# Output projection, norm and first feed-forward products of a two-layer backbone, by halves of the tokens

## The chip, the cores and the metric

The kernel runs on one core of a Trainium2 chip. The metric is the time of one execution on the device in microseconds (us); before the change it is 2305.74 us (median of three runs, 2302.88 to 2308.2).

## What is computed

Two layers over 512 latent tokens and 256 context tokens of width D = 1024, in float32. Layer 0 mixes tokens by attention, layer 1 by a bidirectional RWKV-7 scan; layer 1 updates the latents alone. Each mixer ends in an output projection `wo`, whose result is added by a gate; then comes a modulated RMS norm and a SwiGLU network (DFF = 2816), added by a gate too. Cut to what matters here:

```python
y, yc = mixer(h, hc, ...)                     # ends in o @ wo, o (tokens, 1024), wo (1024, 1024)
x = x + m[:, 2] * y
h2 = rmsnorm(x, norm2_g[i]) * (1.0 + m[:, 4]) + m[:, 3]
x = x + m[:, 5] * ((silu(h2 @ wg) * (h2 @ wu)) @ wd)
# layer 0: the same for the context tokens, with their own modulation
```

## The kernel before

Features lie on the 128 partitions, tokens along a row: `xT` is [128, 8 feature tiles k, tokens], and a copy of it is kept in DRAM (`xd`). Every product is made of three float32r passes, of high and low parts (xh wh, xl wh, xh wl), so a weight block [128, 4, 128] becomes a "unit": a raw tile `wr` (0.5 MB loads of line 249 on SyncE's queue, SP, four buffers), a CAST to the high part on ScalarE (ACT, line 239) and a difference for the low part (line 241), which goes to VectorE (DVE), for every third unit to GpSimd (POOL). Seven units can be held.

The part that is changed runs once per layer. It starts when the mixer's output stands in SBUF as `oTh`, `oTl` (line 726 is attention's last cast):

- `out_project` (from line 264) forms wo^T o in eight feature tiles, all tokens of a tile before the next one (the two streams of 512 and 256 tokens apart; the last two tiles by halves of the tokens). Line 228 is the matmul, 258 adds by the gate on DVE, 277 writes to `xd`.
- `squares` (lines 176, 178) sums x * x over the feature tiles, for either half of the tokens; line 186 sums over partitions by matmul, 158 to 165 form the inverse root, 194 and 197 spread it over the partitions (`rbp`).
- `norm_blocks` (from line 300) multiplies by the inverse norm (314, DVE), modulates (322 on ACT for the first half of the tokens, 320 on POOL for the second), and forms the seven token blocks of a Strassen-Winograd product: B11 and B21 of the first half (x1, x2), B22 and T1 to T4, which need both halves (x3 to x7). Their sums are 336, 339, 341 and 344, each over four feature tiles, on POOL; 329 and 330 split each block into high (ACT) and low (DVE) parts.
- `ffn` (from line 349) takes pairs of feature tiles b = 0 to 10: `gate_up(b)` makes the seven products of gate and up weights (line 395, in the order 1, 2, 5, 6, 7, 3, 4, in PSUM tiles A, B, C); sums of weight blocks are line 360 on POOL; 383 to 404 combine products on DVE and ACT, with Silu at 404. `down` (429) follows one pair behind.

Half n2 is 384 tokens in layer 0 and 256 in layer 1. A list scheduler puts the instructions of each engine in their order when the kernel is built; each engine then runs its own list in order, as SP does with its loads. The output projection is called at line 744 (layer 0, after the load of `xT` at 736) and 1408 (layer 1); `mods`, a pool of two 1 MB tiles `mw`, holds the modulation weights that are loaded during attention (line 123).

## Time and profile before

| | |
|---|---|
| median of three runs | 2305.74 us (2302.88 to 2308.2) |
| span of the profiled execution | 2302.6 us; its time outside the span isn't recorded, and the span is 3.1 us below the median |
| busy share PE, DVE, ACT, POOL | 88%, 73%, 48%, 34% |
| chain that ended last: PE, DVE | 63%, 20% |
| layer 0, end of attention to the second pair's products | 429.5 to 600.1 us |
| layer 1, end of the readout to the second pair's products | 1863.3 to 2004.8 us |

PE is TensorE's matmuls. The chain is the row of pieces that ended last, followed back from the last instruction; a window gives each engine's busy time in one stretch, with the granted clock of TensorE as a share of its full 2.4 GHz. In a timeline, what stands in brackets is the idle time of the engine before the instruction and what ended it. One execution is profiled, so durations come from that one.

### The profile page before, as it was taken

The page shows a single profiled execution, that of the slowest core. Times are in us where ns is not written, and L with a number is a line of the kernel's source. Part 1 is how long each engine was busy: PE and PEld are TensorE (multiplying, and loading weights), DVE is VectorE, ACT ScalarE, POOL GpSimd, SP SyncE. Part 2 cuts the span into 40 slices and gives each one's busy share as a digit, 9 for nine tenths or more (in the row PEclk, how much of TensorE's full clock was granted, in tenths as well). Part 3 has the DMA queues.
Part 4 walks back from the last instruction along what each step waited for, and adds up shares of the span by engine and source line. Part 5 has one row for each costly group of instructions (what it writes and reads, how often), then busy time and mean ns, then how long its engine had stood idle before and what let it go on. Part 6 is the DMA issues. An engine that isn't in the chain of part 4 may idle for free.

```text
span 2302.6 us, 42745 instructions
## 1 busy us (share of the span) xinstructions
PE 2034.6 (88%) x16422; PEld 1779.6 (77%) x16422; DVE 1669.9 (73%) x3382; ACT 1094.9 (48%) x2276; POOL 790.8 (34%) x663
## 2 busy tenths in 40 slices
PE   6999999797999999995988978767888777899998
PEld 4995555586999999994767956656777666899998
DVE  4565556449877777768465597798888758988896
ACT  5446656434333333335343764765664534444443
POOL 1110000027434443423142531552430325666661
PEclk7999999998999999997988979778889987999999
DMA  8206660421321222111326543432321631433332
GB/s 298 67 25 222 237 237 21 148 91 48 109 74 63 74 68 74 62 55 64 100 88 211 148 121 120 121 107 64 110 62 54 189 121 47 138 97 97 105 97 74
DMA packets 178714, 247.94 MB, mean 108 GB/s; under 512 B 16808, under 2 KB 109968, under 8 KB 178128
## 3 DMA queue, kind: packets, MB, share of 16 engines
q1 hardware_dynamic: 177792, 244.37, 33.0%
q8 instruction: 130, 2.13, 0.4%
q10 hardware_dynamic: 352, 0.60, 0.1%
q0 software_dynamic: 368, 0.26, 0.1%
q14 instruction: 72, 0.59, 0.1%
HBM read 199.04 MB, written 33.55 MB: 101 GB/s over the span
## 4 chain that ended last, share of the span: by engine, by line
PE 63%; DVE 20%; ACT 5%; issue 5%; DMA 4%; POOL 2%; SPq 1%; DVEq 0%; ACTq 0%; POOLq 0%
PE yps L429 13%; PE A L395 8%; PE C L395 5%; PE B L395 5%; PE yps L228 5%; PE po L724 3%; DVE O L1144 3%; PE pj L228 3%; PE S L705 2%; DVE E L1147 2%; PE PTp L719 2%; PE mps L126 2%; DVE wu L241 2%; PE qps L578 2%; PE qps L580 2%
## 5 line engine op out<-in xcount | busy, mean ns | idle before, releaser
L429 PE MATMUL yps<-gh,wu 128*128 128x384 f32 (+2 forms) x1120 | 323.4, 345 | 3.7 <-DVE xT L258 3.6
L258 DVE SCALAR_TENSOR_TENSOR xT<-yps,modT,xT 128x384 f32<-128x384 f32 (+2 forms) x348 | 183.9, 548 | 134.1 <-PE yps L429 95.0
L241 POOL TENSOR_TENSOR wu<-wr,wu 128x512 fp32r<-128x512 f32 x77 | 107.1, 1392 | 472.6 <-ACT wu L239 456.9
L239 ACT CAST wu<-wr 128x512 fp32r<-128x512 f32 x252 | 154.6, 620 | 222.2 <-PE A L395 66.4
L429 PEld LDWEIGHTS yps<-gh,wu 128*128 128x128 f32 x1120 | 201.6, 188 | 16.5 <-DVE xT L258 4.7
L239 ACT CAST wu<-ws 128x512 fp32r<-128x512 f32 x176 | 108.0, 620 | 200.2 <-PE yps L429 86.5
L241 DVE TENSOR_TENSOR wu<-wr,wu 128x512 fp32r<-128x512 f32 x175 | 157.7, 903 | 50.8 <-ACT wu L239 47.8
L429 PE MATMUL yps<-gl,wu 128*128 128x384 f32 (+2 forms) x560 | 192.1, 344 | 0.0
L360 POOL TENSOR_TENSOR ws<-wr 128x512 f32<-128x512 f32 x88 | 130.1, 1482 | 165.8 <-DMA wr<-in_ffn_wg_dram 71.5
L241 DVE TENSOR_TENSOR wu<-ws,wu 128x512 fp32r<-128x512 f32 x111 | 125.8, 1139 | 9.8 <-ACT wu L239 9.8
L241 POOL TENSOR_TENSOR wu<-ws,wu 128x512 fp32r<-128x512 f32 x65 | 88.1, 1356 | 90.3 <-ACT wu L239 87.6
L429 PEld LDWEIGHTS yps<-gl,wu 128*128 128x128 f32 x560 | 105.4, 188 | 4.5
L228 PE MATMUL yps<-oTh,wu 128*128 128x512 f32 (+2 forms) x416 | 101.6, 347 | 8.2 <-ACT wu L239 8.2
L708 DVE TENSOR_REDUCE mx<-S 128x1 f32<-128x768 f32 (+1 forms) x96 | 74.7, 778 | 44.4 <-PE S L705 43.7
L720 ACT COPY PT<-PTp 128x384 f32<-128x384 f32 (+1 forms) x160 | 69.3, 465 | 54.0 <-PE PTp L719 53.8
L395 PE MATMUL C<-x5h,wu 128*128 128x384 f32 (+1 forms) x352 | 85.6, 318 | 6.0 <-ACT x5h L329 5.2
L719 PEld LDWEIGHTS PTp<-ident,pr 128*128 128x128 f32 x448 | 50.2, 144 | 50.5 <-issue 23.6
L395 PE MATMUL A<-x1h,wu 128*128 128x384 f32 (+1 forms) x352 | 88.0, 315 | 1.1 <-ACT x1h L329 1.1
L395 PE MATMUL B<-x2h,wu 128*128 128x384 f32 (+1 forms) x352 | 83.8, 310 | 4.7 <-ACT x2h L329 4.6
L1147 DVE TENSOR_TENSOR E<-E,O 128x110 f32<-128x110 f32 (+22 forms) x288 | 84.2, 325 | 0.3
L395 PE MATMUL A<-x6h,wu 128*128 128x384 f32 (+1 forms) x352 | 83.1, 314 | 1.0 <-DVE wu L241 1.0
L1144 DVE TENSOR_TENSOR O<-E 128x110 f32<-128x110 f32 (+22 forms) x288 | 82.4, 322 | 1.9
(408 smaller groups left out, 6365.4 us busy)
## 6 DMA issues: line engine op xcount, KB each, us to landing
mw<-in_mod_w_dram SPq DMA_DIRECT2D x48, 1024.0 KB, 5.3
wr<-in_ffn_wg_dram SPq DMA_DIRECT2D x44, 512.0 KB, 3.8
wr<-in_ffn_wu_dram SPq DMA_DIRECT2D x44, 512.0 KB, 3.6
wr<-in_ffn_wd_dram SPq DMA_DIRECT2D x44, 512.0 KB, 3.9
wraw<-in_rwkv_wrkv_dram SPq DMA_DIRECT2D x32, 256.0 KB, 3.1
wraw<-in_attn_wqkv_dram SPq DMA_DIRECT2D x12, 512.0 KB, 4.5
xT<-xd SPq DMA_DIRECT2D x2, 3072.0 KB, 9.8
AR<-lw SPq DMA_DIRECT2D x48, 128.0 KB, 2.3
```

The lines of the kernel that those rows point to most:

```text
L228: nc.tensor.matmul(ps, w(k), x(k, sl), start=(k == 0 and i == 0), stop=(k == nk - 1 and i == 2))
L239: nc.scalar.copy(hi, raw)
L241: (nc.gpsimd if lane["n"] % 3 == 0 else nc.vector).tensor_tensor(out=lo, in0=raw, in1=hi, op=ALU.subtract)
L258: nc.vector.scalar_tensor_tensor(out=xT[:, f, t0:t1], in0=ps[:, t0 - sl.start:t1 - sl.start], scalar=modT[:, l, 8 * m + f, s:s + 1], in1=x ...
L360: nc.gpsimd.tensor_tensor(out=t, in0=x, in1=y, op=op)
L395: nc.tensor.matmul(ps, w[:, k], x[:, k], start=(k + j == 0), stop=(k == 3 and j == 2))
L429: nc.tensor.matmul(ps, u[k // 2][w][:, k % 2, fs], gs[k // 2][x][:, k % 2, sl], start=(k + j == 0), stop=(k == nk - 1 and j == 2))
L708: nc.vector.tensor_reduce(out=mx, in_=S[:, :nk * P], axis=AX.X, op=ALU.max)
L719: nc.tensor.transpose(ps[:, t - t0, :], pr_[:, P * t:P * t + P], ident)
L720: nc.scalar.copy(PT[h][:, t0:t1, P * qt:P * qt + P], ps[:, :t1 - t0, :])
L1144: nc.vector.tensor_tensor(out=tv, in0=E[:, a_:b, s:s + 1].to_broadcast([P, b - a_, m]), in1=E[:, s:s + 1, :s].to_broadcast([P, b - a_, m]) ...
L1147: nc.vector.tensor_tensor(out=E[:, a_:b, :s], in0=E[:, a_:b, :s], in1=tv, op=ALU.add)
```

## The change

- The projection runs by halves of the tokens: eight feature tiles of the first half, then eight of the second (`out_half`). Weights are loaded and cast again for the second half.
- In layer 0 the weights of the first two blocks (2 x 1 MB) are loaded through the modulation weights' buffers, on SP ahead of the load of `xT`.
- `norm_half` norms the first half of the tokens and splits x1 and x2 beside the second half's projection. For the second half, modulation is on ACT (it was on POOL), and the token sums are on DVE, in pieces of one (line 323) or two feature tiles (333).
- `gate_first` runs products 1 and 2 of the pairs b = 0 and 1 (8 x 12 = 96 matmuls), which need the first half alone, behind the projection; their weights come in 256 KB loads. `gate_up` makes the other five products. All PSUM tiles are in one pool.

```diff
-    def out_project(wp, pl, xT, src, xh, xl, l, m, n):
...
+    def out_half(wp, pf, xT, src, xh, xl, l, m, sl, ready=None):
+        tags = [f"{z}{y}" for z in "ABC" for y in range(2)]
+        w = sl.stop - sl.start
         for b in range(4):
...
+            rw_ = (ready or {}).get(b) or raws(wp, src, 256 * b, 256)
+            for q in range(2):
                 f = 2 * b + q
...
+                us = [unit(wp, r[:, :, P * q:P * q + P], (4, P)) for r in rw_]
+                ps = pf.tile([P, 512], F32, name="yps", tag=tags[f % 6])[:, :w]
+                product([(ps, sl)], lambda k: us[k // 4][0][:, k % 4], lambda k: us[k // 4][1][:, k % 4], xh, xl, KT)
+                add_gated(xT, ps, l, m, f, sl)
+                nc.sync.dma_start(out=xd[:, f, sl], in_=xT[:, f, sl])
...
-    def norm_blocks(pool, pf, xT, sums, l, w, xv, n):
...
+    def norm_half(pool, pf, xT, th, l, w, xv, n):
...
+        sl = slice(n2 * th, n2 * th + n2)
+        acc = squares(pool, xT, sl, abufs=2, bufs=2)
+        ps = pf.tile([P, 512], F32, name="rbp", tag=f"D{th}")
+        r = rms_cols(pool, ps[:, 508:512], [acc], nt)
...
+        rb = ps[:, :n2]
+        if th:
+            preload(AF.Silu, r[:, 0:1])
...
-                        if th:
-                            nc.gpsimd.tensor_scalar(out=h[:, k, t0:t1], in0=h[:, k, t0:t1], scalar1=a_, scalar2=b_, op0=ALU.mult, op1=ALU.add)
-                        else:
-                            nc.scalar.activation(h[:, k, t0:t1], h[:, k, t0:t1], AF.Identity, bias=b_, scale=a_)
...
-        nc.gpsimd.tensor_tensor(out=B11, in0=B12, in1=B11, op=ALU.subtract)
-        parts(5, B11, 2)
...
+        def normed(k):
+            nc.vector.tensor_tensor(out=xT[:, k, sl], in0=xT[:, k, sl], in1=rb, op=ALU.mult)
+            for s, off, wd in STREAMS:
+                t0, t1 = max(off, sl.start), min(off + wd, sl.stop)
+                if t0 < t1:
+                    nc.scalar.activation(xT[:, k, t0:t1], xT[:, k, t0:t1], AF.Identity, bias=modT[:, l, 8 * m + k, s:s + 1],
+                                         scale=aT[:, 2 * l + w, k, s:s + 1])
...
+        if th == 0:
+            for k in range(KT):
+                normed(k)
+                parts(1 + k // 4, (B11, B21)[k // 4], k % 4, k % 4 + 1)
+            return
+        for k in range(4):
+            normed(k)
+            nc.vector.tensor_tensor(out=B11[:, k], in0=B12[:, k], in1=B11[:, k], op=ALU.subtract)
+            parts(5, B11, k, k + 1)
+        for k in range(4):
+            normed(4 + k)
+        two = [slice(0, 2), slice(2, 4)]
+        for i, o, x, y in ((6, B11, B22, B11), (7, B12, B22, B12), (4, B21, B21, B11)):
...
+            for z in two:
+                nc.vector.tensor_tensor(out=o[:, z], in0=x[:, z], in1=y[:, z], op=ALU.subtract)
+                parts(i, o, z.start, z.stop)
...
+        def gate_first(b):
+            st = half_tiles(b, b % 2)
+            st["get"] = [first_blocks(z, b) for z in (wg, wu)]
+            gate_steps(st, ORDER[:2])
+            return st
...
+        ahead = [gate_first(b) for b in range(2)]
         for b in range(nb):
-            gs.append(gate_up(b))
+            gs.append(gate_up(b, ahead[b] if b < 2 else None))
...
+            ready = {}
+            for b in range(2):
+                raw = md.tile([P, KT, 256], F32, name="mw", tag="mw", bufs=2)
+                nc.sync.dma_start(out=raw, in_=a["attn_wo"][0].rearrange("(k p) f -> p k f", p=P)[:, :, 256 * b:256 * b + 256])
+                ready[b] = [raw[:, 0:4], raw[:, 4:8]]
...
+            for th in range(2):
+                out_half(wp, pf, xT, a["attn_wo"][0], lambda k, sl: oTh[:, k, sl], lambda k, sl: oTl[:, k, sl], 0, 2,
+                         slice(n2 * th, n2 * th + n2), None if th else ready)
...
+                norm_half(tp, pf, xT, th, 0, 1, xv, T)
```

TensorE, layer 0, behind the projection (`yps`); `acc` and `sq` are the sums of squares of half 1, `x1h` to `x2l` parts of half 0:

```order
L228 MATMUL yps<-oTh,wu 128x384
L186 MATMUL rbp<-ones,acc 128x1
L186 MATMUL rbp<-ones,sq 128x1
...
L197 MATMUL rbp<-dg,ones 128x128 x6
L395 MATMUL A_5360<-x1h,wu 128x384
L395 MATMUL A_5377<-x1h,wu 128x384
```

```order
L395 MATMUL A_5446<-x1h,wu 128x384 x2
L186 MATMUL rbp<-ones,sq 128x1
...
L395 MATMUL A_5446<-x1l,wu 128x384
...
L395 MATMUL A_5513<-x1h,wu 128x384 x2
L197 MATMUL rbp<-dg,ones 128x128 x3
L395 MATMUL A_5513<-x1l,wu 128x384
```

Before (first piece) both halves' sums and spreads stood ahead of all products; now (second piece) the sums and the spread of half 1 stand inside the first products.

SP's queue, layer 0, at the load of the projection's weights, before and then after:

```order
L123 DMA mw<-in_mod_w_dram 128x4x512 x40
L736 DMA xT<-xd 128x6144
L249 DMA wr<-in_attn_wo_dram 128x4x256 x8
L277 DMA xd<-xT 128x512
L277 DMA xd<-xT 128x256
```

```order
L707 DMA mw<-in_attn_wo_dram 128x8x256 x2
L759 DMA xT<-xd 128x6144
L249 DMA wr<-in_attn_wo_dram 128x4x256 x4
L275 DMA xd<-xT 128x384 x2
L249 DMA wr<-in_attn_wo_dram 128x4x256
L275 DMA xd<-xT 128x384
```

Two loads of the projection's weights moved ahead of the load of `xT`; the others now stand between the writes of `xd`.

ACT, layer 1, at the inverse norm (`rs_y` is the square root), before and then after:

```order
L176 ACTIVATE sq<-xT 128x256 x3
L158 ACTIVATE rs_y<-rbp,epst 128x2 x2
L153 ACT_TABLE_LOAD
L153 ACTIVATE idle<-rr,epst 128x1
L322 ACTIVATE xT<-xT,modT,aT 128x256 x2
```

```order
L239 CAST wu<-wr 128x512
L404 ACT_TABLE_LOAD
L404 ACTIVATE gt<-gt 128x256
L158 ACT_TABLE_LOAD
L158 ACTIVATE rs_y<-rbp,epst 128x2
L239 CAST wu<-ws 128x512
L398 COPY gt<-A_20170 128x256
L153 ACT_TABLE_LOAD
```

The first Silu of the feed-forward network moved ahead of half 1's square root, with a table load on either side.

## Rows read from the trace of the kernel before

**Rows 1.** The page: busy time, share of the span and instructions of each engine, and the chain that ended last, by engine.

```profile
PE 2034.6 (88%) x16422; PEld 1779.6 (77%) x16422; DVE 1669.9 (73%) x3382; ACT 1094.9 (48%) x2276; POOL 790.8 (34%) x663
...
PE 63%; DVE 20%; ACT 5%; issue 5%; DMA 4%; POOL 2%; SPq 1%; DVEq 0%; ACTq 0%; POOLq 0%
```

**Rows 2.** Windows of layer 0, from the start of the projection on: start:end, its us, then busy us and count of PE, of PE's weight loads, DVE, ACT and POOL, the granted clock as a share, the busy share of the DMA engines and GB/s.

```profile
437.65:506.80 69.15, 69.14 (x387) 62.39 (x387) 29.06 (x41) 19.57 (x35) 16.95 (x12) 0.98 0.36 119
506.80:531.20 24.40, 16.78 (x79) 15.85 (x80) 18.26 (x44) 14.94 (x27) 13.87 (x18) 0.72 0.17 52
531.20:560.10 28.90, 15.88 (x74) 14.28 (x73) 28.32 (x16) 10.54 (x18) 22.96 (x10) 0.82 0.00 1
```

**Rows 3.** The chain of work that ended last, in order of time, 420 to 605 us: start, duration, what.

```profile
425.98 10.98 DMA wr<-in_attn_wo_dram
...
524.90 3.08 POOL xT L320 x5
...
548.83 3.56 DVE x7l L330 x2
552.67 6.19 DVE x6l L330 x2
...
583.48 4.16 PE A L395 x24
```

**Rows 4.** The products of line 395 alone, from the end of attention to the second pair's products in layer 0: the window, its us, PE busy and count, then weight loads, clock, DMA.

```profile
429.50:600.12 170.62, 64.63 (x336) 61.59 (x336) 0.91 0.34 114
```

**Rows 5.** The same chain in layer 1, in its steady stretch.

```profile
2002.59 1.38 PE yps L429 x6
...
2007.62 2.83 PE B L395 x24
```

**Rows 6.** The same windows in layer 1, for line 395 (first row) and line 429 (second).

```profile
1863.27:2004.80 141.53, 58.58 (x410) 55.89 (x411) 0.91 0.29 94
...
1863.27:2004.80 141.53, 12.79 (x48) 8.42 (x48) 0.91 0.29 94
```

**Rows 7.** Window of layer 1's projection, all engines (columns as in rows 2).

```profile
1863.27:1908.73 45.46, 45.46 (x245) 38.89 (x244) 20.03 (x32) 15.07 (x29) 12.82 (x10) 0.99 0.31 102
```

**Rows 8.** Timeline of ACT, then of PE, at the start of layer 0's projection.

```profile
429.51 0.37 ACT L726 CAST oTh<-po 128x256 fp32r<-128x256 f32 x1 [1.17 <-PE po L724]
436.98 0.62 ACT L239 CAST wu<-wr 128x512 fp32r<-128x512 f32 x1 [7.10 <-DMA wr<-in_attn_wo_dram]
...
437.65 1.01 PE L228 MATMUL yps<-oTh,wu 128*128 128x512 f32 x2 [8.18 <-ACT wu L239]
```

**Rows 9.** Timeline of SP's queue from 330 us to the end of attention (the first two rows): start, time that the issues took, loads.

```profile
334.73 14.98 SPq L123 DMA_DIRECT2D mw<-in_mod_w_dram  x4
425.59 0.34 SPq L736 DMA_DIRECT2D xT<-xd  x1
```

**Rows 10.** Timeline of DVE, layer 0.

```profile
514.47 7.52 DVE L314 TENSOR_TENSOR xT<-xT,rbp 128x384 f32<-128x384 f32 x16 [0.41 <-PE rbp L197]
...
528.39 0.96 DVE L330 TENSOR_TENSOR x3l<-xT,x3h 128x768 fp32r<-128x768 f32 x1 [2.13 <-ACT x3h L329]
531.11 7.97 DVE L330 TENSOR_TENSOR x3l<-xT,x3h 128x768 fp32r<-128x768 f32 x1 [1.76 <-ACT x3h L329]
539.00 0.68 DVE L241 TENSOR_TENSOR wu<-ws,wu 128x512 fp32r<-128x512 f32 x1
539.60 0.54 DVE L400 TENSOR_TENSOR gt<-gt,B 128x384 f32<-128x384 f32 x1
...
565.56 1.01 DVE L400 TENSOR_TENSOR gt<-gt,C 128x384 f32<-128x384 f32 x2
```

**Rows 11.** Timeline of POOL, layer 0 and, in the last row, layer 1.

```profile
530.18 3.47 POOL L336 TENSOR_TENSOR xT<-xT 128x1536 f32<-128x1536 f32 x1
...
534.84 3.43 POOL L341 TENSOR_TENSOR xT<-xT 128x1536 f32<-128x1536 f32 x1
...
565.05 1.30 POOL L241 TENSOR_TENSOR wu<-wr,wu 128x512 fp32r<-128x512 f32 x1 [7.00 <-DMA wr<-in_ffn_wu_dram]
...
1935.86 2.49 POOL L339 TENSOR_TENSOR xT<-xT 128x1024 f32<-128x1024 f32 x1 [0.63 <-DVE x5l L330]
```

**Rows 12.** Timeline of ACT: layer 0 (high part, modulation), then layer 1 (a table load and what follows it).

```profile
516.27 0.50 ACT L329 CAST x1h<-xT 128x384 fp32r<-128x384 f32 x1
...
517.69 1.90 ACT L322 ACTIVATE xT<-xT,modT,aT 128x384 f32<-128x384 f32 x3
...
1915.21 1.28 ACT L153 ACT_TABLE_LOAD   x1
1916.51 0.29 ACT L153 ACTIVATE idle<-rr,epst 128x1 f32<-128x1 f32 x1
```

**Rows 13.** Loads of the projection's weights between 430 and 500 us: KB of each, median us from issue to landing.

```profile
wr<-in_attn_wo_dram SPq DMA_DIRECT2D x5, 512.0 KB, 5.0
```

**Rows 14.** Timeline of DVE, layer 1.

```profile
1919.65 0.41 DVE L330 TENSOR_TENSOR x1l<-xT,x1h 128x256 fp32r<-128x256 f32 x1
1919.99 2.40 DVE L314 TENSOR_TENSOR xT<-xT,rbp 128x256 f32<-128x256 f32 x7
...
1936.04 4.56 DVE L330 TENSOR_TENSOR x7l<-xT,x7h 128x512 fp32r<-128x512 f32 x2
```

**Rows 15.** Window of most of layer 1's scan (columns as in rows 2).

```profile
1170.00:1700.00 530.00, 433.28 (x5024) 365.33 (x5024) 425.66 (x961) 306.46 (x666) 213.43 (x211) 0.85 0.41 121
```

More of the change, by code (lines that the diff above doesn't have):

```diff
@@ L272, in tile_ @@
                 f = 2 * b + q
-                outs = [(pl.tile([P, 512], F32, name="yps", tag="yps", bufs=6)[:, :sl.stop - sl.start], sl) for sl in sls]
-                product(outs, lambda k: us[q][k // 4][0][:, k % 4], lambda k: us[q][k // 4][1][:, k % 4], xh, xl, KT)
-                for ps, sl in outs:
-                    add_gated(xT, ps, l, m, f, sl)
-                    nc.sync.dma_start(out=xd[:, f, sl], in_=xT[:, f, sl])
-            if b < 3:
-                for q in range(2):
-                    tile_(q, [slice(off, off + w) for _, off, w in STREAMS if off < n])
-            else:
-                for sl in halves:
-                    for q in range(2):
-                        tile_(q, [sl])
+                us = [unit(wp, r[:, :, P * q:P * q + P], (4, P)) for r in rw_]
@@ new lines, in parts @@
+        def parts(i, src, k0, k1):
+            hi, lo = (z[:, k0:k1] for z in xv[i])
+            nc.scalar.copy(hi, src[:, k0:k1])
+            nc.vector.tensor_tensor(out=lo, in0=src[:, k0:k1], in1=hi, op=ALU.subtract)
+        B11, B12, B21, B22 = (xT[:, 4 * kh:4 * kh + 4, n2 * t:n2 * t + n2] for kh in range(2) for t in range(2))
+        if th == 0:
[3 more added lines that the diff above has]
+            return
@@ new lines, in norm_half @@
+        for k in range(4):
[6 more added lines that the diff above has]
+        for i, o, x, y in ((6, B11, B22, B11), (7, B12, B22, B12), (4, B21, B21, B11)):
+            if i == 4:
+                for z in two:
+                    parts(3, B22, z.start, z.stop)
+            for z in two:
+                nc.vector.tensor_tensor(out=o[:, z], in0=x[:, z], in1=y[:, z], op=ALU.subtract)
+                parts(i, o, z.start, z.stop)
@@ L385, in finish @@
                 nc.vector.tensor_tensor(out=gl[o], in0=g, in1=gh[o], op=ALU.subtract)
-            for i in ORDER:
+            for i in order:
                 for y in range(2):
-                    wh, wl = get[y](i)
+                    wh, wl = st["get"][y](i)
                     z = on[i]
@@ L406, in gate_up @@
                             finish(c)
-            return gh, gl
+        def gate_first(b):
[3 more added lines that the diff above has]
+            return st
+        def gate_up(b, st=None):
+            order = ORDER[2:] if st else ORDER
+            st = st or half_tiles(b, 0)
+            st["get"] = [blocks(z, b) for z in (wg, wu)]
+            for y in range(2):
+                for z in ("21", "22"):
+                    st["t"][y][z] = tp.tile([P, n2], F32, name="gt", tag=f"{z}{y}")
+            gate_steps(st, order)
+            return st["gh"], st["gl"]
         def down(b0, gs, tags, last=None):
@@ L671, in layer0 @@
             return True
+        md = pool(mods, "md", side="right")
         os_ = ExitStack()
```

116 lines of the change are left out of this document (38 added, 78 removed).

## The prediction

> **What bounds the kernel now.** I read the page first: TensorE (PE) is busy for 88% of the span and the chain of work that ended last runs through it for 63%, through VectorE (DVE) for 20% [rows 1]. So a gain is time in which PE waits, and the question is how much of that lies where the change works. The windows of layer 0 tell it [rows 2]: PE runs full in the projection (69.14 of 69.15 us), then in the two windows from 506.8 to 560.1 us it is busy for 32.7 of 53.3 us, at a granted clock of 0.72 and 0.82. The chain names who holds it up [rows 3]: a load of the projection's weights ahead of it, then GpSimd (POOL) at the modulation of line 320, and DVE at x7l and x6l; late in the stretch the chain is PE itself.
>
> How much is lost is worked out by counting. A steady group of 24 matmuls of 384 columns takes 4.16 us, 0.1733 each [rows 3]. From the end of attention at 429.5 to 600.12 us PE did the projection, which is 384 matmuls at that width (66.5 us), and 336 products, two pairs of 168 [rows 4] (58.2 us). That is 124.7 us of work in 170.6 us: **45.9 us lost**. The same for layer 1, where 24 matmuls of 256 columns take 2.83 us (0.118 each) and six of 512 columns of the down product 1.38 us (0.23 each) [rows 5]: from 1863.27 to 2004.80 us (141.5 us) lie a projection worth 384 x 0.118 = 45.3 us, 410 products (48.4 us) and 48 down matmuls (11.0 us) [rows 6]: **36.8 us lost**, nearly all of it after the projection's end at 1908.73, since the window of the projection is full [rows 7].
>
> **The early weights (layer 0).** PE's first projection matmul waited 8.18 us for a weight cast, which waited 7.10 us for the load; attention's last cast on ScalarE (ACT) was done at 429.88 [rows 8]. Two 1 MB loads now stand on SP's queue right behind the modulation weights', whose last issue was over by 349.7, and the queue then had nothing until 425.59 [rows 9]: the loads land long before they are used. Left are the last cast of attention's output, a difference on DVE (0.7 us) and one weight pair at most: PE starts at about 431, so 1.5 us stay of 8.2. PE then hardly goes idle; the first two projection matmuls of 512 columns took 1.01 us [rows 8], against 0.46 for two at the steady pace of [rows 5], so that part of the 69.15 - 66.5 = 2.6 us over the ideal goes with the gap.
>
> **The projection by halves** has the same 384 matmuls' columns, but casts its weights twice: 16 more units per layer and eight more 0.5 MB loads. A unit costs 0.62 on ACT and 0.68 on DVE or 1.3 on POOL [rows 8, 10, 11]. In layer 0 that is 10 us more for ACT and some 7 for DVE; half 0's norm adds 8 x (0.63 + 0.50) on ACT and 8 x (0.47 + 0.54) on DVE [rows 10, 12]. DVE was busy for 29.1 and ACT for 19.6 of 69 us there [rows 2], so they come to about 45 and 39, and POOL has room: hidden, at zero to 2 us. A block of weights is now used up in 8.3 us (layer 1: 5.7) where a load takes 5.0 from issue to landing [rows 13] and runs up to two blocks ahead. If that cover were gone, each load would show whole (a rival below).
>
> **First products as cover.** Behind the projection PE has 96 products of half 0 that need nothing of half 1: 96 x 0.1733 = 16.6 us in layer 0, 11.3 in layer 1, and half 0's spread sums sit inside the second half's products.
>
> **The chain behind half 1, layer 0.** The projection ends at 431 + 66.5 + 2 = 500, the covered products at 517. The sums over partitions stand some 33 products in (506), the spread of the inverse norm some 65 in, so the eight products with it start on DVE at 511.6. From there to the last x4l the instructions in DVE's new order are: 8 x 0.47, 4 token sums x 0.54, 6 of double length x 0.96, 4 parts x5l x 0.54, 8 parts x 0.96, 5 weight differences x 0.68, 4 combinations x 0.54 [rows 10]: 27.2 us, done by 539. PE wants x5l at 517 and gets its first three slices at about 523; after that it is never further behind than these 6 us, since x4 would be due at 533.7 and is taken slice by slice. Modulation on ACT is eight pairs of 128 and 256 columns, between 8 x 0.63 = 5 us (as one of 384) and 16 x 0.63 = 10 [rows 12]; I take 8, nearer the upper end since a short one still has its fixed part, and it runs beside DVE. **Stall 6.**
>
> **POOL beside DVE.** The same difference of 768 columns took 0.96 us before POOL's token sums began, and 7.97 us while POOL ran two of 3.4 us [rows 10, 11]; x6l took 6.19 for two [rows 3]. Combinations that read one operand from PSUM kept their 0.5 us beside a weight difference on POOL [rows 10, 11]. The four token sums leave POOL, but weight sums and a third of the weight differences stay there, some 8 x 1.3 = 10.4 us in the 27 us above. The cost lies between 0 and 10; I take 5, as about half of them meet a DVE instruction with two operands in SBUF. The Trainium skill, page "SBUF — State Buffer", section "Who interferes with whom", says that a DVE instruction with two SBUF inputs contends with a GpSimd instruction that reads SBUF, and that whoever comes first blocks the other fully; the rows agree (7.97 against 0.96). By it the sums now put on DVE are just the exposed kind: with full blocking the term would be about 8 per layer, without any 0, so the total would move by +6 or -10 us.
>
> **Layer 0 together:** left are 1.5 (start), 2 (sums and spread), 6 and 5, or 14.5 of 45.9: gain 31, between 22 (stalls at 20) and 39 (at 3).
>
> **Layer 1.** No early load is made, and its start had no gap. The projection ends at about 1909.5, the cover at 1920.9. Before half 1's inverse norm ACT now has a table load with a Silu, then a load for Sqrt, then Silu's again behind it: two loads more than before, 1.28 us each by the row, with the next operation 1.30 after its start [rows 12]. The Trainium skill, "ScalarE: Activation LUTs", section "What ACT_TABLE_LOAD costs", gives some 2.7 us for a switch with its drain, which would add 2.8 us to this chain; the row shows no such drain. DVE starts the eight products at about 1920 and has 8 x 0.34 + 7 x 0.68 + 4 x 0.41 + 4 x 0.41 + 6 x 0.68 + 4 x 0.41 + 8 x 0.68 = 21.9 us to the last x4l (0.68 is the weight difference's time, which has the same 512 columns; the others have 256) [rows 10, 14], so 1942, where PE would want x4 at 1932. Stall 7, POOL beside DVE 5 (x7l took 4.56 for two beside POOL's 2.49 [rows 11, 14]), later hitches 3, sums 1.5: 16.5 of 36.8 stay. **Gain 20**, between 10 and 30.
>
> **The scan.** The new order of layer 1's mixer differs in places on every engine, though nothing was rewritten there; its window has 530 us with PE busy for 433 [rows 15]. Start and end hold the same instructions. I take 0, and +-6 (6% of its 97 idle us) for the range. Other edits cost nothing on the path: the reload of xT and the writes to xd are on SP's queue ahead of nothing that is short, and two of the first blocks' loads have half-length rows but 8 us of time.
>
> **Sum.** 31 + 20 = 51 us off the profiled span of 2302.6 gives 2251.6. The span lies 3.1 us under the median of 2305.7, so the median becomes **2255 us**.
>
> **Rivals.** (a) *DVE becomes the bound*: the stalls are at their upper ends (POOL's blocking in full, the in-order sums behind weight differences), gains 22 and 10 less some later hitches, some 27 in all: about 2278. For it: DVE is busy for 28.3 of 28.9 us in the worst window [rows 2]. Against: there it sits in stretched instructions. (b) *The cover is complete*: only the start and the sums remain, 39 + 33: about 2233. Against it is the count of 27 us on DVE against 16.6 of cover. (c) *The change doesn't do what it says*: PE stands in order behind a sum or spread placed too early among the first products (it waits there for ACT's squares of the last tile), so the cover buys nothing, and what is gained is the start (6.6) and POOL's sums (some 8): about 2291. (d) *Slower: the doubled weight stream.* If each load shows, because it stands on SP's queue behind a write of xd that waits for DVE, then 6 + 8 = 14 blocks lose 5.0 us of landing: 70 us, against 51 gained, about 2325. It decides from 3.6 us shown per block. Against it: before, the loads stood behind the same writes and PE was full. The rest is for a scan that comes out much worse.
>
> **Chances.** Forecast (2236 to 2274) 0.62, (a) 0.16, (b) 0.07, (c) 0.07, (d) 0.04, the scan 0.04, which leaves no difference (0.03) or a loss (0.01). A difference of 0.2% (4.6 us) is about what a measurement of this kernel can tell from no change. Faster: 0.62 + 0.16 + 0.07 + 0.07 = 0.92; within it 0.03; slower 0.05. The range of 2236 to 2282 holds the forecast and most of (a), eight in ten.
>
> **What would show it.** Right: PE's first projection matmul within 2.5 us of attention's last; the clock at 1.0 through the first products; one stall of 5 to 12 us at x5 in layer 0 and one of 8 to 16 in layer 1; x7l, x6l and x4l near 1 us each where POOL is quiet. Wrong: gaps inside the second half of the projection that end at a weight load or cast (d), PE waiting at the sums (c), two-part differences still at 4 us and more (a), or a scan window more than 6 us off 530.

## The result and the profile after

The changed kernel takes 2287.65 us (median of five runs, 2281.48 to 2295.33); the kernel before took 2306.75 beside it (five runs, 2302.88 to 2309.76). The ratio is 0.9918, with a 95% interval of 0.9894 to 0.9941: 19 us faster, where 51 were forecast. The time lies 5.7 us above the range.

The page of the changed kernel, with the lines that answer to [rows 1] (busy time and share of the span, then the chain that ended last):

```profile
span 2279.8 us, 43273 instructions
...
PE 2024.0 (89%) x16566; PEld 1785.4 (78%) x16566; DVE 1694.4 (74%) x3439; ACT 1128.5 (49%) x2338; POOL 787.6 (35%) x642
...
PE 63%; DVE 21%; DMA 5%; ACT 4%; issue 4%; POOL 2%; SPq 0%; DVEq 0%; POOLq 0%; ACTq 0%
```

The profiled span is 22.8 us shorter than before (the profiled execution is the fastest of the five). To see where, I cut both spans at the same matmuls: attention's last, the mixer's first (`pj`), and the readout's last.

| stretch | before, us | after, us | change | forecast |
|---|---|---|---|---|
| to the end of attention | 429.1 | 427.9 | -1.2 | 0 |
| layer 0: projection and feed-forward network | 639.2 | 618.0 | -21.2 | -31 |
| layer 1's mixer with its scan | 794.9 | 804.8 | +9.9 | 0 |
| layer 1: projection and feed-forward network | 439.4 | 429.1 | -10.3 | -20 |

So in this profile a third of what is missing lies in the mixer, where nothing was rewritten, and a third in each layer.

**Layer 0.** Windows of the changed kernel, from attention's last cast to the second pair's products (columns as in [rows 2]):

```profile
428.30:429.24 0.94, 0.00 (x1) 0.00 (x1) 0.44 (x2) 0.94 (x3) 0.00 (x0) 1.00 0.99 418
429.24:498.20 68.96, 68.86 (x402) 68.53 (x403) 46.36 (x82) 38.41 (x70) 18.71 (x12) 1.00 0.63 199
498.20:517.00 18.80, 18.80 (x116) 18.64 (x114) 10.79 (x22) 10.34 (x21) 11.28 (x8) 1.00 0.29 89
517.00:545.00 28.00, 18.28 (x88) 16.73 (x88) 27.84 (x40) 18.11 (x34) 16.52 (x6) 0.82 0.26 78
545.00:573.60 28.60, 27.31 (x156) 26.55 (x155) 25.74 (x35) 12.19 (x24) 18.24 (x12) 1.00 0.54 198
```

Its timeline of PE, at the start, at the projection's end and at the two waits of the fourth window:

```profile
427.18 1.08 PE L747 MATMUL po<-PT,vt 128*64 128x256 f32 x6 [0.46 <-ACT PT L743]
429.24 0.45 PE L228 MATMUL yps<-oTh,wu 128*128 128x384 f32 x1 [0.98 <-ACT wu L239]
...
498.13 0.34 PE L228 MATMUL yps<-oTh,wu 128*128 128x384 f32 x1
...
523.51 1.01 PE L395 MATMUL C<-x5h,wu 128*128 128x384 f32 x2 [6.35 <-ACT x5h L312]
...
527.37 0.69 PE L395 MATMUL C<-x5l,wu 128*128 128x384 f32 x1 [2.85 <-DVE x5l L313]
```

The projection starts 0.98 us behind attention's last matmul where it waited 8.18 [rows 8], runs full, and the first products follow at full clock. Then PE waits for x5, and DVE is busy for 27.84 of 28.00 us. By the prediction's own method, the 145.3 us hold 66.5 of projection and 336 products at 0.1733, which are 58.2: 20.6 us lost, where 45.9 were before and 14.5 were forecast. From the second pair on to the mixer the layer takes 472.7 us against 468.75 before, so 4 of the 25.3 gained are given back there; 2.1 of them are one wait for a weight difference on POOL.

**Layer 1.** Windows of the changed kernel, from the projection on, to the same 48 matmuls of the down product as in [rows 6]:

```profile
1850.80:1896.40 45.60, 45.60 (x399) 45.60 (x399) 34.98 (x68) 29.74 (x62) 13.34 (x10) 0.99 0.63 190
1896.40:1908.00 11.60, 10.49 (x89) 10.09 (x88) 7.82 (x19) 8.14 (x14) 3.17 (x4) 1.00 0.65 208
1908.00:1930.00 22.00, 9.59 (x57) 8.90 (x56) 19.72 (x36) 13.62 (x30) 18.14 (x9) 0.70 0.17 49
1930.00:1963.00 33.00, 29.76 (x220) 28.02 (x219) 30.30 (x49) 14.98 (x31) 20.38 (x15) 0.94 0.51 163
1963.00:1990.00 27.00, 25.13 (x167) 23.14 (x166) 22.54 (x33) 11.84 (x23) 18.96 (x13) 0.94 0.32 97
```

Its waits of PE from 1896 to 1990 us: who waited for what, us in total, times, the longest:

```profile
PE C L395 <- ACT x5h L312: 6.0, 1, 6.0
PE A L395 <- ACT x6h L312: 3.6, 1, 3.6
PE C L395 <- DVE x5l L313: 2.8, 1, 2.8
PE A L395 <- ACT wu L239: 1.9, 1, 1.9
```

The projection is full (45.60 of 45.60) in spite of its doubled weight stream. The 139.2 us hold 45.3 of projection, 464 products at 0.118 (54.8) and 48 down matmuls at 0.23 (11.0): 28.1 lost, of 36.8 before, where 16.5 were forecast to stay.

**Who is late at x5 and x6.** Timeline of the changed kernel on DVE (layer 0), then on POOL (layers 0 and 1):

```profile
511.33 1.11 DVE L241 TENSOR_TENSOR wu<-ws,wu 128x512 fp32r<-128x512 f32 x1 [1.83 <-ACT wu L239]
512.36 1.65 DVE L385 TENSOR_TENSOR gl<-gt,gh 128x384 fp32r<-128x384 f32 x1
513.93 3.79 DVE L303 TENSOR_TENSOR xT<-xT,rbp 128x384 f32<-128x384 f32 x8
...
518.25 2.55 DVE L323 TENSOR_TENSOR xT<-xT 128x384 f32<-128x384 f32 x3
...
522.73 3.51 DVE L333 TENSOR_TENSOR xT<-xT 128x768 f32<-128x768 f32 x2
...
540.95 0.94 DVE L313 TENSOR_TENSOR x4l<-xT,x4h 128x768 fp32r<-128x768 f32 x1
```

```profile
533.87 10.43 POOL L241 TENSOR_TENSOR wu<-ws,wu 128x512 fp32r<-128x512 f32 x2 [8.44 <-ACT wu L239]
...
1919.31 7.87 POOL L349 TENSOR_TENSOR ws<-wr,ws 128x512 f32<-128x512 f32 x1 [3.17 <-DVE wu L241]
```

A combination of the first products (`gl`) and a weight difference stand in DVE's row ahead of the eight products with the inverse norm, and run stretched. While POOL forms a weight difference and sums weights, three token sums take 2.55 us and two double ones 3.51 (0.54 and 0.94 each alone). Later it is the other way: DVE runs back to back at 0.94 each, and POOL's two weight differences take 10.43 (1.3 each in [rows 11]). In layer 1 a weight sum on POOL takes 7.87. Who waits for it shows in the timeline of ACT, layer 1:

```profile
1901.36 1.28 ACT L404 ACT_TABLE_LOAD   x1
1902.66 0.42 ACT L404 ACTIVATE gt<-gt 128x256 f32<-128x256 f32 x1
1903.09 1.28 ACT L158 ACT_TABLE_LOAD   x1
1904.39 0.26 ACT L158 ACTIVATE rs_y<-rbp,epst 128x2 f32<-128x2 f32 x1
...
1927.21 0.62 ACT L239 CAST wu<-ws 128x512 fp32r<-128x512 f32 x1 [6.27 <-POOL ws L349]
1927.73 1.13 ACT L312 CAST x6h<-xT 128x512 fp32r<-128x512 f32 x2
```

ACT stands for 6.27 us at the cast of that sum; x6h comes behind it in ACT's row, and PE waits 3.6 for x6h. (The first four rows are the table loads that the prediction spoke of.)

### The profile page after: what moved, and what is told of

Same layout as the page of the kernel before. It is cut to its first block, busy times and chain, and to the rows that moved or that the text cites. A ratio compares the mean times of both kernels' runs of the same rounds, so it can differ in the third digit from the quotient of the medians.

```text
span 2279.8 us, 43273 instructions
## 1 busy us (share of the span) xinstructions
PE 2024.0 (89%) x16566; PEld 1785.4 (78%) x16566; DVE 1694.4 (74%) x3439; ACT 1128.5 (49%) x2338; POOL 787.6 (35%) x642
## 4 chain that ended last, share of the span: by engine, by line
PE 63%; DVE 21%; DMA 5%; ACT 4%; issue 4%; POOL 2%; SPq 0%; DVEq 0%; POOLq 0%; ACTq 0%
PE yps L445 13%; PE A L395 8%; PE B L395 5%; PE C L395 5%; PE yps L228 5%; DVE O L1167 3%; PE po L747 3%; PE S L728 2%; PE pj L228 2%; DVE E L1170 2%; PE PTp L742 2%; PE mps L126 2%; PE qps L595 2%; PE qps L597 2%; PE qps L596 2%
## 5 line engine op out<-in xcount | busy, mean ns | idle before, releaser
L258 DVE SCALAR_TENSOR_TENSOR xT<-yps,modT,xT 128x384 f32<-128x384 f32 (+3 forms) x360 | 185.2, 537 | 124.7 <-PE yps L445 105.9
L239 ACT CAST wu<-wr 128x512 fp32r<-128x512 f32 x276 | 168.5, 619 | 171.6 <-PE A L395 56.6
L241 POOL TENSOR_TENSOR wu<-wr,wu 128x512 fp32r<-128x512 f32 x86 | 123.8, 1439 | 241.2 <-ACT wu L239 217.6
L241 DVE TENSOR_TENSOR wu<-wr,wu 128x512 fp32r<-128x512 f32 x190 | 161.8, 857 | 12.9 <-ACT wu L239 12.4
L241 DVE TENSOR_TENSOR wu<-ws,wu 128x512 fp32r<-128x512 f32 x111 | 135.5, 1221 | 22.2 <-ACT wu L239 22.0
L241 POOL TENSOR_TENSOR wu<-ws,wu 128x512 fp32r<-128x512 f32 x65 | 100.1, 1540 | 66.1 <-ACT wu L239 65.9
L228 PE MATMUL yps<-oTh,wu 128*128 128x384 f32 (+1 forms) x512 | 110.9, 309 | 1.1 <-ACT wu L239 1.0
L395 PE MATMUL C<-x5h,wu 128*128 128x384 f32 (+1 forms) x352 | 85.0, 319 | 14.5 <-ACT x5h L312 12.3
L1167 DVE TENSOR_TENSOR O<-E 128x110 f32<-128x110 f32 (+22 forms) x288 | 87.9, 341 | 2.2
L395 PE MATMUL A<-x1h,wu 128*128 128x384 f32 (+1 forms) x352 | 83.1, 311 | 4.5 <-POOL wu L241 2.1
L228 PEld LDWEIGHTS yps<-oTh,wu 128*128 128x128 f32 x512 | 85.4, 189 | 1.9 <-ACT wu L239 1.4
```

The costliest lines, as they stand in the source:

```text
L228: nc.tensor.matmul(ps, w(k), x(k, sl), start=(k == 0 and i == 0), stop=(k == nk - 1 and i == 2))
L239: nc.scalar.copy(hi, raw)
L241: (nc.gpsimd if lane["n"] % 3 == 0 else nc.vector).tensor_tensor(out=lo, in0=raw, in1=hi, op=ALU.subtract)
L258: nc.vector.scalar_tensor_tensor(out=xT[:, f, t0:t1], in0=ps[:, t0 - sl.start:t1 - sl.start], scalar=modT[:, l, 8 * m + f, s:s + 1], in1=x ...
L395: nc.tensor.matmul(ps, w[:, k], x[:, k], start=(k + j == 0), stop=(k == 3 and j == 2))
L1167: nc.vector.tensor_tensor(out=tv, in0=E[:, a_:b, s:s + 1].to_broadcast([P, b - a_, m]), in1=E[:, s:s + 1, :s].to_broadcast([P, b - a_, m]) ...
```

## The experiments

The kernels ran on several chips; each ratio is to the kernel before on the same chip. Two ratios that differ by under about 0.003 (7 us) are not told apart, as each has an interval of some +-0.002. Differences in us between two kernels are taken from their ratios.

**The mixer's order.** In the first, the changed kernel, each engine's instructions of layer 1's mixer are tied to the order that they had before; in the second, the kernel before, they are tied to the changed order. The ties add no work to any engine: they only fix the row.

```diff
+    m0 = len(nc.cur_bb.bb.instructions)
...
+        row = [ins[k + d] for k, d in enumerate(shifts)]
+        for x, y in zip(row, row[1:]):
+            tc.add_manual_dep(y, x.name, mybir.DependencyInfo(mybir.DependencyClass.NoSync, mybir.DependencyReason.DATA), reason="order")
```

> The changed kernel, with one thing altered: on each engine the instructions of layer 1's mixer (from its first line to the end of the readout) are tied by order-only edges to the row in which they stood before the change; nothing else moves but two instructions. Theory 1 (the list order of the scan costs the 10 us by which the mixer came out longer, 812.4 us from the first projection matmul of the mixer to the end of the readout, now 804.9 instead of 794.9): the mixer takes 795 us again and the kernel about 2277 us, 10 less than the changed kernel's 2287.7. Theory 2 (the mixer's extra time is scatter between executions or comes from what the memory does, and its order is worth nothing): 2287 us, mixer 805.

> The mirror image: the kernel before, with layer 1's mixer tied to the row that the changed kernel gives it, all else as before. Theory 1: the mixer takes about 805 us instead of 795, the kernel about 2317 us, 0.4% slower than before. Theory 2: no difference from before, 2306 us.

Measured: 2281.43 us, ratio 0.9886 (0.9872 to 0.99), against 0.9918 without the ties; and 2316.27, ratio 1.004 (1.0027 to 1.0053). The changed order costs the kernel before 9 us (6 to 12); undoing it gives the changed kernel some 7 (1 to 14). As one tie costs and the other gains, the tying itself is not the cause. All further kernels hold the order of before, so the ones that carry both layers' change are compared with 0.9886. Windows of the whole mixer, of the kernel before and then of the changed kernel:

```profile
1068.30:1863.20 794.90, 639.77 (x7606) 543.90 (x7607) 610.65 (x1373) 429.75 (x913) 266.98 (x259) 0.86 0.37 113
```

```profile
1045.90:1850.70 804.80, 641.15 (x7605) 546.84 (x7606) 614.73 (x1371) 429.42 (x913) 267.85 (x260) 0.86 0.38 112
```

PE's work is the same (641 against 640 us), and PE idles for 8.5 us more. The mixer's time in one profile doesn't size the effect: fifteen profiles of kernels with the order of before gave 792 to 806 us, and neither tied kernel's mixer took the 795 or 805 that was expected. The same windows of the tied kernels, the changed one in the old order and then the one before in the changed order:

```profile
1048.85:1849.82 800.97, 649.22 (x7607) 552.17 (x7607) 608.19 (x1371) 429.81 (x913) 268.99 (x260) 0.84 0.38 112
```

```profile
1068.21:1880.05 811.84, 650.73 (x7607) 556.17 (x7607) 611.16 (x1372) 428.36 (x913) 263.62 (x259) 0.85 0.38 111
```

PE's idle time (the window less PE's busy time) does tell the orders apart: 149.7 to 155.1 us in the fifteen profiles with the order of before, 163.7 and 161.1 in the two with the changed one. What scatters between profiles of one order is mostly PE's busy time for the same matmuls, 639 to 651 us at a granted clock of 0.86 to 0.84.

**Each layer alone.** One layer with `out_half`, `norm_half` and `ffn` as changed, the other with the functions of before:

```diff
+        norm_blocks(tp, pf, xT, sums, 1, 1, xv, L)
...
+        ffn_old(pf, xT, 1, xv, L, wp, tp, gp, 1, halves)
```

> Layer 0's projection, norm and feed-forward network as changed, layer 1's as before, the mixer tied to the order of before. Theory 1: 2306.7 less 21 to 22, about 2285 us, and with the 10.5 of layer 1 that makes the 2275 to 2277 of the changed kernel with the old mixer. Theory 2 (layer 0's gain was as forecast, 31): 2276 us.

> Layer 0 as before, layer 1's projection, norm and feed-forward network as changed; the mixer stands in the order of before without being tied. It gives what the change is worth in layer 1 alone. Theory 1 (the parts add up: layer 0 gives 21, layer 1 gives 10.5, the mixer takes 10 back): 2296 us, 0.45% faster. Theory 2 (layer 1's gain was as forecast, some 20, and is hidden in one disturbed execution): 2287 us.

Measured: layer 0 alone 2285.1 us, ratio 0.9906 (0.9893 to 0.9918), or 21.7 us; layer 1 alone 2301.47, ratio 0.9979 (0.9968 to 0.999), or 5 us (2 to 7). The two make 26.5, and the changed kernel with the mixer's order of before gains 26.3: the parts add up. Less the mixer's 9 they make 17, near the 19 measured. Layer 1's part is the one that came out furthest below its forecast of 20, and below both theories of this run.

**Parts of the change undone.** Each starts from the changed kernel with the mixer's order of before.

```diff
-                nc.sync.dma_start(out=raw, in_=a["attn_wo"][0].rearrange("(k p) f -> p k f", p=P)[:, :, 256 * b:256 * b + 256])
...
-                         slice(n2 * th, n2 * th + n2), None if th else ready)
+                         slice(n2 * th, n2 * th + n2))
```

> The changed kernel with the mixer in the old order (2281.4 us), without the two early loads of the projection's weights: all blocks are loaded by halves as the rest. Theory 1 (the start is worth what it showed, an idle time of 8.2 us that became 1.0): 2288 to 2289 us, idle before the first projection matmul about 8 us. Theory 2 (what starts late is made up behind the projection, where VectorE sets the pace): 2281 to 2283.

Measured: 2288.97 us, ratio 0.9918 (0.9901 to 0.9936), 7 us slower. Its timeline of PE shows the wait of [rows 8] again:

```profile
436.54 0.69 PE L295 MATMUL yps<-oTh,wu 128*128 128x384 f32 x1 [8.46 <-ACT wu L306]
```

```diff
-            nc.vector.tensor_tensor(out=B11[:, k], in0=B12[:, k], in1=B11[:, k], op=ALU.subtract)
+            nc.gpsimd.tensor_tensor(out=B11[:, k], in0=B12[:, k], in1=B11[:, k], op=ALU.subtract)
...
-                nc.vector.tensor_tensor(out=o[:, z], in0=x[:, z], in1=y[:, z], op=ALU.subtract)
+                nc.gpsimd.tensor_tensor(out=o[:, z], in0=x[:, z], in1=y[:, z], op=ALU.subtract)
```

> The changed kernel with the mixer in the old order (2281.4 us), the token sums T1 to T4 again on GpSimd (in the new small pieces), all else as changed. Theory 1 (GpSimd and VectorE hold each other up whenever both read SBUF, so sums on GpSimd stretch VectorE's differences to several us again and wait themselves): 4 to 8 us more per layer, 2290 to 2297 us. Theory 2 (VectorE's amount of work sets the pace, 4 + 6 sums of 0.55 and 0.94 us are better off it): 3 us less per layer, 2275.

Measured: 2294.45 us, ratio 0.9936 (0.9916 to 0.9955), 11.5 slower: the token sums are better on DVE. The last x4l is done 57.1 us behind layer 0's projection, against 43.4 in the changed kernel.

```diff
-        ahead = [gate_first(b) for b in range(2)]
...
-            gs.append(gate_up(b, ahead[b] if b < 2 else None))
+            gs.append(gate_up(b))
```

> The changed kernel with the mixer in the old order (2281.4 us), without the early products: the pairs b = 0 and 1 make all their seven products one after the other. Half 0 of the norm still runs beside the projection. Theory 1 (the pair b = 1's 48 products are cover that is missing between the pair b = 0's products 1, 2 and 5; b = 0's own still stand ahead): 8.3 us more in layer 0 and 5.7 in layer 1, 2295 us. Theory 2 (VectorE's row sets the time and not the cover, and without the first pair's extra combinations and table loads in it x5 comes earlier): 2281 to 2286.

Measured: 2279.38 us, ratio 0.9876 (0.9858 to 0.9895). Without the second pair's early products the kernel is no slower that can be told. Its waits of PE in layer 0, from 495 to 545 us, then its timeline of PE (the projection's end) and of DVE (the last x4l):

```profile
PE C L462 <- ACT x5h L379: 10.0, 1, 10.0
```

```profile
501.81 0.34 PE L295 MATMUL yps<-oTh,wu 128*128 128x384 f32 x1
...
536.62 0.95 DVE L380 TENSOR_TENSOR x4l<-xT,x4h 128x768 fp32r<-128x768 f32 x1
```

PE waits 10.0 us instead of 6.35 + 2.85, since x5 is ready sooner: the eight products with the inverse norm start 12.1 us behind the projection instead of 15.5, and the last x4l is done at 35.4 instead of 43.4. (Products 1 and 2 of the first pair still run behind the projection here, where their pair stands, so half of the cover is left; what that half is worth was not tried.)

**The chain put ahead in the rows.** The next two keep the first products and tie instructions behind others in their engine's row: first weight differences and combinations behind the eight products and x5 on DVE and ACT; then the sums and spread of half 1 ahead of the ninth and the 25th of the first products on PE.

```diff
+            if lane["n"] % 3:
+                behind(x, mark["rb"])
...
+                    behind(x, mark[5][1])
+                    behind(y, mark[5][0])
```

> The changed kernel with the mixer in the old order (2281.4 us), and order-only edges in both layers: the first products' Silu, gating and split (lines 404, 383 to 385) stand behind the last piece of x5 on ScalarE and VectorE, and VectorE's first weight differences of the pair b = 0's sums stand behind the eight products of half 1 with the inverse norm. Layer 1's two extra table loads are gone with that. Theory 1 (the chain behind half 1 is late because VectorE and ScalarE, each in its row, wait there for weights, table loads and first-product work): x5 comes 3 to 4 us earlier in layer 0 and 5 to 6 in layer 1, 2272 to 2274 us. Theory 2 (VectorE's amount of work, and its collisions with GpSimd, set the time; what is moved back is missing later): 2280 to 2283.

```diff
+                                if mark["n"] > 8:
+                                    behind(x_, mark["sum"])
+                                if mark["n"] > 24:
+                                    behind(x_, mark["spread"])
```

> The changed kernel with the mixer in the old order (2281.4 us), and order-only edges on TensorE alone, in both layers: half 1's sums over partitions stand behind the first 8 of the early products (before: 33 in layer 0), the spread of the inverse norm behind the first 24 (before: 65). The scheduler, seeing this, also drops layer 1's two extra table loads. Theory 3 (the early products stand ahead of the sums and the spread in TensorE's row, so that they delay the chain behind half 1 by as much as they cover: the eight products of half 1 with the inverse norm began 15.5 and 14.0 us behind the projection's end, against 7.7 and 7.3 before the change): they begin at 5 to 8 us, x5 at 15 to 19 instead of 25 and 20, the kernel gains 6 to 9 us in layer 0 and 4 to 6 in layer 1: 2267 to 2271 us. Theory 4 (VectorE's amount of work between the projection and the second pair sets the time, wherever the chain starts): x5 comes earlier but x4 no earlier than now (48 and 44 us behind the projection), 2279 to 2283 us.

Measured: 2286.09 us, ratio 0.99 (0.9882 to 0.9919), and 2284.15, ratio 0.9897 (0.9877 to 0.9918): no gain from either, though in the second the eight products start 6.3 us behind the projection, 9 sooner. Its timeline of DVE, layer 0, then one row of POOL's:

```profile
504.69 3.80 DVE L377 TENSOR_TENSOR xT<-xT,rbp 128x384 f32<-128x384 f32 x8 [1.02 <-PE rbp L264]
508.42 1.63 DVE L309 TENSOR_TENSOR wu<-ws,wu 128x512 fp32r<-128x512 f32 x1
509.97 1.65 DVE L397 TENSOR_TENSOR xT<-xT 128x384 f32<-128x384 f32 x1
...
512.00 2.75 DVE L397 TENSOR_TENSOR xT<-xT 128x384 f32<-128x384 f32 x2
...
516.24 4.02 DVE L407 TENSOR_TENSOR xT<-xT 128x768 f32<-128x768 f32 x2
520.18 1.76 DVE L309 TENSOR_TENSOR wu<-ws,wu 128x512 fp32r<-128x512 f32 x1
...
540.81 0.95 DVE L387 TENSOR_TENSOR x4l<-xT,x4h 128x768 fp32r<-128x768 f32 x1
```

```profile
509.45 3.31 POOL L423 TENSOR_TENSOR ws<-ws,wr 128x512 f32<-128x512 f32 x2
```

Sooner, the chain runs into all of POOL's weight sums: from 508.4 to 534 many rows take two to three times their 0.54, 0.68 and 0.94, some 11 us more in all, and the last x4l is done as late as before (43.4 behind the projection).

**Two smaller suspects.** The weight sums of the first pair on DVE instead of POOL, with the sums early and without:

```diff
-                nc.gpsimd.tensor_tensor(out=t, in0=x, in1=y, op=op)
+                (nc.vector if b == 0 else nc.gpsimd).tensor_tensor(out=t, in0=x, in1=y, op=op)
```

> As the run before (sums and spread early in TensorE's row), and the eight sums of weight blocks of the pair b = 0 (line 349 of the changed kernel) on VectorE instead of GpSimd. Theory 5 (GpSimd starves beside VectorE's row of two-operand instructions: one sum of 1.3 us took 7.9 in layer 1, and ScalarE's row stood behind it): 3 to 5 us less in layer 1 and about 0 in layer 0 against the run before. Theory 4 (VectorE's amount of work sets the time): 8 x 0.68 = 5.4 us more per layer, some 10 us more than the run before.

> The changed kernel with the mixer in the old order (2281.4 us), the eight sums of weight blocks of the pair b = 0 on VectorE in both layers, without the early sums of the norm. Theory 5 (GpSimd's starvation holds ScalarE's row and with it x6): 3 to 5 us less in layer 1, 2277. Theory 4 (VectorE's amount of work sets the time): 5 us more per layer, 2291.

Measured: 2286.37 us, ratio 0.9911 (0.9892 to 0.993), and 2278.99, ratio 0.9872 (0.985 to 0.9895): no gain that can be told from none. DVE now has the sums' work itself, its products start later (12.6 and 18.4 us behind layer 0's projection), and in a row that runs in order it is held by what the sums wait for.

The Silu of the first products tied behind the table load of half 1's root, so that ACT loads two tables fewer; last, with the weight sums on DVE as well:

```diff
-                            nc.scalar.activation(t[c], t[c], AF.Silu)
+                            x = nc.scalar.activation(t[c], t[c], AF.Silu)
+                            if i == 2:
+                                behind(x, mark["silu"])
```

> The changed kernel with the mixer in the old order (2281.4 us), and one order-only edge per layer: the first Silu stands behind the preload of its table, so that layer 1's two extra table loads (1.28 us each) are gone. Theory 1 (they lie on the chain behind half 1's norm): 2.5 us less, 2279. Theory 2 (the chain waits for TensorE's row or VectorE anyway): 2281.

> The two edits that came out fastest so far together: the changed kernel with the mixer in the old order, the first Silu behind its table's preload (2276.9 us alone) and the eight weight sums of the pair b = 0 on VectorE (2279.0 alone). If both gains are real and add up: 2274 us. If what is seen of them lies within the scatter of the mixer (its time differed by 10 us between profiles with the same order): 2276 to 2281.

Measured: 2276.9 us, ratio 0.9868 (0.9845 to 0.9891), and 2276.18, ratio 0.9871 (0.9852 to 0.9889). Against 0.9886 neither gain is certain, and they don't add. These are the fastest kernels that compute the whole result: some 30 us under the kernel before, and 11 under the changed one, of which some 7 are the mixer's order and the rest is not told from none.

**POOL kept quiet.** The weight sums of the first two pairs left out, first in the changed kernel, then with the sums early in PE's row:

```diff
             def summed(i, x, y, op):
+                if b < 2:
+                    sums[i] = x
+                    return x
```

> The changed kernel with the mixer in the old order (2281.4 us), the chain starting as there at some 15 us, and GpSimd's sums of weight blocks left out for the pairs b = 0 and 1 (raw blocks in their place). Theory 6 together with theory 3 (both the late start and the stretching count, and either alone hides the other): x4l some 42 us behind layer 0's projection, nearly as now, since the chain begins at 14 to 15 and needs 27; 2276 to 2281 us. If GpSimd's sums alone were the cause, it would be as fast as the run beside it (2262 to 2272).

> As the run with half 1's sums and spread early in TensorE's row (2284.2 us; the chain began 6.3 us behind layer 0's projection instead of 15.5, yet the last x4l came at 43.4 as without it), but GpSimd's sums of weight blocks are left out for the pairs b = 0 and 1 of both layers (the raw blocks are used in their place), so that GpSimd is nearly still while VectorE works off the chain. Theory 6 (VectorE's two-operand instructions were stretched by GpSimd's weight sums, some 11 us of them in layer 0): VectorE's row is done in 27 us plus two or three, the last x4l stands at 33 to 37 us behind layer 0's projection and at 32 to 36 in layer 1, and the kernel takes 2262 to 2272 us. Theory 4 (VectorE's own amount of work sets it): the last x4l stays at 41 to 44, 2279 to 2284 us.

Measured: 2265.11 us, ratio 0.9828 (0.9815 to 0.9841), 13 less than with the sums; and 2254.26, ratio 0.9774 (0.976 to 0.9787), 28 less than the early chain with the sums. So an early chain gains some 12 us, but only where POOL is quiet. The first run missed its expectation (2276 to 2281), which held that a late chain hides what POOL costs: it doesn't. Timeline of DVE in the last kernel, layer 0:

```profile
503.91 3.81 DVE L377 TENSOR_TENSOR xT<-xT,rbp 128x384 f32<-128x384 f32 x8 [1.02 <-PE rbp L264]
507.63 0.69 DVE L309 TENSOR_TENSOR wu<-wr,wu 128x512 fp32r<-128x512 f32 x1
508.23 1.65 DVE L397 TENSOR_TENSOR xT<-xT 128x384 f32<-128x384 f32 x1
...
510.27 1.01 DVE L397 TENSOR_TENSOR xT<-xT 128x384 f32<-128x384 f32 x2
...
512.15 0.94 DVE L407 TENSOR_TENSOR xT<-xT 128x768 f32<-128x768 f32 x1
```

The token sums are at their own times again but one (1.65, beside a weight difference, of which POOL still has a few). The last x4l is done 35.9 us behind the projection, and PE no longer waits for x5. Windows of 498 to 545 us, of the kernel with the early chain and the weight sums, then of this one:

```profile
498.00:545.00 47.00, 37.55 (x187) 35.12 (x187) 43.18 (x57) 27.96 (x53) 20.81 (x14) 0.85 0.28 84
```

```profile
498.00:545.00 47.00, 42.45 (x231) 41.06 (x230) 41.99 (x71) 32.03 (x62) 10.91 (x6) 0.93 0.42 142
```

PE gets 44 more matmuls done, and DVE 14 more instructions in less busy time. What was left out is more than the delay of DVE by POOL: a unit no longer waits for its sum either. How the 13 and 28 us divide between the two wasn't tried by itself.

## Why the prediction was wrong

**Right in mechanism and size.** The early weights (6.6 forecast, some 7 by undoing them, between 2 and 13); the doubled weight stream hidden behind a full projection, so rival (d) is out; half 0's norm hidden; no gap at layer 1's start; the clock at 1.0 through the first products. x7l, x6l and x4l took 0.94 each in layer 0, though not because POOL was quiet: two weight differences lay beside most of them there and took 10.43. (In layer 1 x6l took 1.76, with POOL's weight work beside it.) The stall with POOL's share was put at 11, and PE idled for 9.7 in that window (28.00 - 18.28); in layer 1 it was 12 against 12.4 (22.00 - 9.59). In layer 0 the last x4l was forecast 39 us behind the projection and 44 with POOL's term, and was done at 43.4; that is in part luck, as the eight products started 3.9 us late (15.5 behind the projection, 11.6 forecast) and the row from there took 28.0 us, not 27.2 + 5. In layer 1 they started 3.4 us late, and the last x4l was done at 40.5, where 32.5, or 37.5 with POOL's term, was forecast.

**The failed step: "The scan ... I take 0, and +-6".** The order of a stretch that the diff doesn't touch cost 9 us by one run and some 7 by the other. The prediction saw that the order differed on every engine, and took that for noise around nothing. The sign could not be worked out from the trace of before; but a new order is a change of its own, and the range for it should have gone past the 6. With the mixer in the old order the kernel takes 2281.4 us, just inside the range. By the runs, the 32 us that are missing from the forecast are 7 to 9 here, 9 in layer 0 (21.7 of 31) and 15 in layer 1 (5 of 20).

**What stays behind the stall, in both layers.** The sums of what would be left had a term for each wait and, but for 3 us in layer 1, none for what follows a wait:

| left, us | layer 0 forecast | layer 0 measured | layer 1 forecast | layer 1 measured |
|---|---|---|---|---|
| start | 1.5 | 0.9 | 0 | 0 |
| projection over its ideal, sums, spread, first products | 2 | 2.5 + 2.2 | 1.5 | 0.3 + 2.8 |
| PE idle at the stall, POOL's share in it | 6 + 5 | 9.7 | 7 + 5 | 12.4 |
| products of that window at the lower clock | 0 | 3.0 | 0 | 2.9 |
| hitches up to the end of the count | 0 | 2.3 | 3 | 9.7 |
| sum | 14.5 | 20.6 | 16.5 | 28.1 |

The measured terms are the windows less the work in them: 88 products are 15.25 us at full clock and took 18.28; 57 in layer 1 are 6.73 and took 9.59. The granted clock in these windows is 0.82 and 0.70; the old stall had 0.72 and 0.82 in [rows 2], and the prediction read them out, but put no term for the low clock beside the stall that it kept. In layer 1 the hitches are the rest: 9.7 where 3 were put. The clock is 0.94 in both later windows, and PE waits there for combinations on DVE (2.2), a weight cast on ACT (1.9) and weight differences (1.0). That these are late because of the rows of DVE and POOL is argued from the waits, not tried by itself. Between the second pair's products and the mixer, layer 0 gives back another 4.

**Of "First products as cover", the second pair's half bought nothing that can be told** (2279.4 us without it, 2281.4 with it), by a road that the prediction half saw. It counted the 16.6 us of cover against a DVE chain of 27 us that was fixed in length. But the cover is in the chain: its combinations and weight units stand in DVE's row ahead of x5, and the weight sums on POOL stretch that row. Take the second pair's out, and the chain ends 8 us sooner (35.4 against 43.4), as much as the second pair's 48 products take (8.3 us). That is the mechanism of rival (a), DVE as the bound, with POOL as its partner; its price of 2278 is near the 2281 of the changed kernel with the mixer's old order. The time itself lies nearest to rival (c), 2291, but not for its reason: at the sums and the spread PE waits 0.6 us at most.

**A theory of mine that fell.** That DVE's own work, or its order, set the stall: moving the chain to the front of the rows brought its start 9 us forward and its end not at all, and moving weight sums from POOL to DVE gained nothing certain. With POOL's weight sums left out the same early chain was 28 us faster. Here the Trainium skill, page "SBUF — State Buffer", section "Who interferes with whom", applies: by its rule that the two engines block each other the token sums on DVE were the exposed kind. The prediction priced that at 8 per layer on DVE; the traces agree with the rule (0.54 us sums at up to 1.65 beside POOL's), and show the other direction too (POOL at 7.87 for a 1.3 us sum), for which the prediction had no term.

**Open.** What in the mixer's new order costs PE its idle time was not traced to one place. How much of what POOL's weight sums cost is the delay beside DVE, and how much the wait for the sums, is not divided. And no kernel here avoids the collision and computes the whole result.

## What to carry to other kernels

Work put in as cover is not free just because its engine is idle: count its units, sums and combinations in the rows of the engines on the chain that it is to cover, and of the engine that delays them (here POOL). When a stall stays, the products behind it and the waits after it stay too, so carry a term for them from the old stall's windows (its granted clock, and the waits behind it). Where a list scheduler sets the order, hold the untouched stretches to their old order before comparing two versions, or a part of the difference belongs to neither.

## What was unexpected in the hardware

- DVE and POOL delay each other either way, and in these rows it was the one beside the other's unbroken row that lost: DVE's 0.54 us sums took up to 1.65 beside POOL's weight sums, and POOL's 1.3 us instructions took 5 to 8 beside an unbroken row of DVE.
- The order of instructions alone moved this kernel by 0.4% (0.27 to 0.53) with no work added.
- A table load cost ACT what its row shows. In the timeline of ACT above, the next operation starts 1.30 us after each load does. The Trainium skill, page "ScalarE: Activation LUTs", section "What ACT_TABLE_LOAD costs", gives some 2.7 us with a drain; the load itself (1.28 us in the rows) agrees with the page, and no drain shows here.
